# Sliding-window unfold (im2col): nine shifted copies built in SBUF and stored with one transfer per tile, in place of three copies and three strided stores

## Chip, cores and metric

The kernel runs on one core of one Trainium2 chip. The metric is device time in microseconds (us) of one execution, lower is better; the figure for a kernel is the median of its runs. The profile is of one further execution, whose own time is given beside the median.

## The reference

The input `x` is float32 of shape 16 x 64 x 32 x 32 (4.19 MB). For each of the 30 x 30 positions of a 3 x 3 window the nine values under the window are written as a column:

```python
def reference(x, kernel_size):
    batch, c, h, w = x.shape
    h_out = h - kernel_size + 1
    w_out = w - kernel_size + 1
    cols = np.zeros((batch, c * kernel_size * kernel_size, h_out * w_out), dtype=np.float32)
    for b in range(batch):
        col_idx = 0
        for i in range(h_out):
            for j in range(w_out):
                patch = x[b, :, i:i + kernel_size, j:j + kernel_size].copy()
                cols[b, :, col_idx] = patch.ravel()
                col_idx += 1
    return cols
```

So for each of the 16 x 64 = 1024 images the output holds nine rows of 900 numbers, and row (ki, kj) is the 30 x 30 block of the image that begins at row ki and column kj. The output is 1024 x 9 x 900 float32, 33.18 MB. Nothing is calculated; the kernel only moves data.

## The kernel before, in words

An image is one SBUF partition. With 128 partitions there are `n_tiles` = 8 tiles, and the loop at line 47 takes them in turn. For each tile:

- line 51 loads 128 images, 4,096 contiguous bytes each, with one DMA issued from ScalarE's queue (`x_tile`, 512 KB);
- lines 56 to 59 make three copies on VectorE. Copy kj takes all 32 rows of the image and the 30 columns from kj on, and writes them as one contiguous run of 960 numbers, `y_tile[:, kj]`;
- lines 61 to 72 issue three stores from SyncE's queue. Any three rows (0, kj), (1, kj), (2, kj) of the output are the same 960 numbers read from offset 0, 30 and 60, so store kj reads three overlapping runs of 900 numbers per partition out of `y_tile[:, kj]` and writes each to its own place in DRAM:

```python
src = _view(y_tile, kj * (H * WO), [part, [WO, K], [1, HO * WO]])
dst = _view(out, rows0 * out_row + kj * pix, [[out_row, P], [K * pix, K], [1, pix]])
nc.sync.dma_start(out=dst, in_=src)
```

A contiguous run in DRAM is therefore 900 numbers, 3,600 bytes, since the row that follows (ki, kj) in DRAM is (ki, kj+1), which belongs to another store.

Each name in the pool `sbuf` has three buffers (line 45). The framework adds the waits: a copy into `y_tile` of tile t waits until the stores of tile t-3 have landed, a load into `x_tile` of tile t waits until VectorE has copied tile t-3, and store kj waits for copy kj alone. Three queues are at work side by side: ScalarE's with 8 loads and nothing else, VectorE with 24 copies, SyncE's with 24 stores.

Of the kernel before, what the change touches and what calls it, by code (L numbers as in the profile page):

```python
# [2 lines left out]

# [4 lines left out]


def _view(ap: bass.AP, extra_offset: int, dims):
    return dataclasses.replace(
        ap,
        offset=ap.offset + extra_offset,
        ap=[[int(s), int(c)] for s, c in dims],
    )


@with_exitstack
def kernel(  # L20
    ctx: ExitStack,
    tc: tile.TileContext,
    x: bass.AP,
    kernel_size,
    out: bass.AP,
):
    nc = tc.nc
    K = int(kernel_size)
    B, C, H, W = x.shape
    HO = H - K + 1  # L30
    WO = W - K + 1
    assert out.shape == (B, C * K * K, HO * WO)

    P = nc.NUM_PARTITIONS
    dt = x.dtype

    assert P % C == 0
    BPT = P // C
    n_tiles = (B + BPT - 1) // BPT

    x_row = H * W
    out_row = K * K * HO * WO
    pix = HO * WO

    sbuf = ctx.enter_context(tc.tile_pool(name="sbuf", bufs=3))

    for t in range(n_tiles):
        rows0 = t * P
        x_tile = sbuf.tile([P, H * W], dt)
        x_src = _view(x, rows0 * x_row, [[x_row, P], [1, H * W]])  # L50
        nc.scalar.dma_start(out=x_tile, in_=x_src)

        y_tile = sbuf.tile([P, K, H, WO], dt)
        part = y_tile.ap[0]
        xpart = x_tile.ap[0]
        for kj in range(K):
            src = _view(x_tile, kj, [xpart, [W, H], [1, WO]])
            dst = y_tile[:, kj]
            nc.vector.tensor_copy(out=dst, in_=src)  # L59

        for kj in range(K):
            src = _view(
                y_tile,
                kj * (H * WO),
                [part, [WO, K], [1, HO * WO]],
            )
            dst = _view(
                out,
                rows0 * out_row + kj * pix,
                [[out_row, P], [K * pix, K], [1, pix]],  # L70
            )
            nc.sync.dma_start(out=dst, in_=src)  # L72


# [1 line left out]
_INS = ['x', 'kernel_size']  # L76
_OUTS = [((16, 576, 900), 'float32')]
#: Inputs that are plain numbers.
_NUMBERS = {'kernel_size': 3}


# [26 lines left out]
```

## Time and profile before

| | us |
|---|---|
| median of 6 runs | 100.39 |
| lowest and highest of them | 99.64, 100.96 |
| the profiled execution, its own time | 100.73 |
| the span of its trace, from the first to the last instruction | 99.0 |

The page of the profile gives the busy time of each engine, the span in 40 equal slices (a digit is a busy share in tenths, 9 is 90% or more), the DMA queues, the chain of work that ended last, the groups of instructions, and the DMA issues with the time from issue to landing. "q1" is the queue of the stores (SyncE), "q10" that of the loads (ScalarE): their megabytes are those of output and input. A DMA is carried out as packets; their time is given as a share of 16 engines over the stretch. Views asked of the trace for a stretch of time give the same lines for that stretch.

### The profile page before, as it was taken

How to read it: one execution, taken by the hardware profiler on the slowest of the kernel's cores; microseconds unless marked ns; L12 is line 12 of the kernel's file. 1: busy time of each engine (PE TensorE's matmuls, PEld its weight loads, DVE VectorE, ACT ScalarE, POOL GpSimd, SP SyncE). 2: the span in 40 equal slices, each digit the busy share in tenths (PEclk: the TensorE clock that was granted, in tenths of full speed). 3: DMA queues.
4: the chain of work that ended last, by engine and by line, in shares of the span. 5: the costliest groups of instructions: out<-in, count | busy, mean ns of one | idle time of the engine just before them, and what ended most of it. 6: DMA issues, size and time to landing. Idle time of an engine off the chain costs nothing.

```text
span 99.0 us, 138 instructions
## 1 busy us (share of the span) xinstructions
DVE 14.2 (14%) x24; POOL 0.2 (0%) x4
## 2 busy tenths in 40 slices
DVE  0397000006000070001500070007000000000000
POOL 0000000000000000000000000000000000000000
DMA  2999999999999999999999999999999999999981
GB/s 76 369 345 325 340 408 413 419 416 399 399 377 409 412 405 399 385 419 413 405 399 403 403 400 400 399 400 403 400 399 402 402 402 400 400 400 402 399 316 47
DMA packets 10752, 37.37 MB, mean 378 GB/s; under 512 B 512, under 2 KB 512, under 8 KB 10752
## 3 DMA queue, kind: packets, MB, share of 16 engines
q1 hardware_dynamic: 9600, 33.18, 86.2%
q10 hardware_dynamic: 1152, 4.19, 11.3%
HBM read 4.19 MB, written 33.18 MB: 378 GB/s over the span
## 4 chain that ended last, share of the span: by engine, by line
DMA 61%; DVE 7%; DVEq 1%; issue 0%; SPq 0%
DMA out_dram<-y_tile 58%; DVE y_tile L59 7%; DMA x_tile<-in_x_dram 3%; DVEq L103 1%; DVEq L59 0%; SPq L72 0%
## 5 line engine op out<-in xcount | busy, mean ns | idle before, releaser
L59 DVE COPY y_tile<-x_tile 128x960 f32<-128x960 f32 x24 | 14.2, 655 | 54.9 <-DMA out_dram<-y_tile 50.9
L89 POOL MEMSET const-bfloat16-1.0<- 128x1 bf16 x1 | 0.1, 101 | 0.0
L89 POOL MEMSET const-uint8-127<- 128x1 uint8 x1 | 0.1, 101 | 0.0
L89 POOL MEMSET const-float32-0.0<- 128x1 f32 x1 | 0.1, 98 | 0.2 <-issue 0.2
L89 POOL MEMSET const-float32-1.0<- 128x1 f32 x1 | 0.1, 98 | 0.0
## 6 DMA issues: line engine op xcount, KB each, us to landing
out_dram<-y_tile SPq DMA_DIRECT2D x24, 1350.0 KB, 18.8
x_tile<-in_x_dram ACTq DMA_DIRECT2D x8, 512.0 KB, 7.9
```

The costliest lines, as they stand in the source:

```text
L59: nc.vector.tensor_copy(out=dst, in_=src)
L89: nc = _bacc.Bacc("TRN2", target_bir_lowering=False, num_devices=1)
L103: with _tile.TileContext(nc) as tc:
```

## The change

The names `tile_im2col_kernel`, `x_tile` and the loads stay. `y_tile` goes. In its place stands `o_tile`, which holds all nine output rows of an image, 8,100 numbers or 32,400 bytes per partition, in the order of the output. Copy ki writes the three rows (ki, 0), (ki, 1), (ki, 2) in one instruction: its source walks three column offsets, 30 rows and 30 columns, its destination is 2,700 contiguous numbers. Copies ki = 0 and 1 are VectorE's, ki = 2 is ScalarE's. One store per tile then takes the whole of `o_tile`. The old code stays under `PLAN == "A"`, which isn't taken.

```diff
-        y_tile = sbuf.tile([P, K, H, WO], dt)
-        part = y_tile.ap[0]
-        xpart = x_tile.ap[0]
-        for kj in range(K):
-            src = _view(x_tile, kj, [xpart, [W, H], [1, WO]])
-            dst = y_tile[:, kj]
-            nc.vector.tensor_copy(out=dst, in_=src)
-        for kj in range(K):
-            src = _view(
-                y_tile,
-                kj * (H * WO),
-                [part, [WO, K], [1, HO * WO]],
-            )
-            dst = _view(
-                out,
-                rows0 * out_row + kj * pix,
-                [[out_row, P], [K * pix, K], [1, pix]],
-            )
-            nc.sync.dma_start(out=dst, in_=src)
+            o_tile = sbuf.tile([P, K * K, HO * WO], dt)
+            part = o_tile.ap[0]
+            xpart = x_tile.ap[0]
+            for ki in range(K):
+                src = _view(
+                    x_tile,
+                    ki * W,
+                    [xpart, [1, K], [W, HO], [1, WO]],
+                )
+                dst = _view(
+                    o_tile,
+                    ki * K * pix,
+                    [part, [pix, K], [WO, HO], [1, WO]],
+                )
+                if ki < 2:
+                    nc.vector.tensor_copy(out=dst, in_=src)
+                else:
+                    nc.scalar.copy(out=dst, in_=src)
+            dst = _view(
+                out,
+                rows0 * out_row,
+                [[out_row, P], [1, out_row]],
+            )
+            nc.sync.dma_start(out=dst, in_=o_tile)
```

Two queues change their order. The first is ScalarE's. Before, it holds the eight loads alone (`DVE_49` is the count of VectorE's finished instructions, a `DMAHW` name is the count of a landed transfer; the numbers behind `x_tile` tell the tiles apart):

```order
L51 DMA x_tile_58<-in_x_dram 128x1024
L51 DMA x_tile_67<-in_x_dram 128x1024
L51 DMA x_tile_76<-in_x_dram 128x1024
L51 DMA x_tile_85<-in_x_dram 128x1024 [waits DMAHW0_49,DVE_49]
L51 DMA x_tile_94<-in_x_dram 128x1024 [waits DMAHW1_49,DVE_49]
L51 DMA x_tile_103<-in_x_dram 128x1024 [waits DMAHW2_49,DVE_49]
```

After, a table load and eight copies stand among the loads (`Activation_49` is the count of ScalarE's own finished instructions):

```order
L81 DMA x_tile_72<-in_x_dram 128x1024
L100 ACT_TABLE_LOAD
L100 COPY o_tile_60<-x_tile_58 128x2700 [waits DMAHW0_49]
L100 COPY o_tile_67<-x_tile_65 128x2700 [waits DMAHW1_49]
L100 COPY o_tile_74<-x_tile_72 128x2700 [waits DMAHW2_49]
L81 DMA x_tile_79<-in_x_dram 128x1024 [waits DVE_49,Activation_49]
L81 DMA x_tile_86<-in_x_dram 128x1024 [waits DVE_49,Activation_49]
L81 DMA x_tile_93<-in_x_dram 128x1024 [waits DVE_49,Activation_49]
L100 COPY o_tile_81<-x_tile_79 128x2700 [waits DMAHW4_49,DMAHW3_49]
L81 DMA x_tile_100<-in_x_dram 128x1024 [waits DVE_49,Activation_49]
```

The fourth load moved from behind the third load to behind ScalarE's first three copies, and a load waits for two engines in place of one.

The second is SyncE's, the queue of the stores. Before, the first stores read:

```order
L72 DMA out_0_dram<-y_tile_60 384x1x900 [waits DVE_49] x2
L72 DMA out_0_dram<-y_tile_60 384x1x900 [waits DMAHW0_49,DVE_49]
L72 DMA out_0_dram<-y_tile_69 384x1x900 [waits DMAHW1_49,DVE_49]
L72 DMA out_0_dram<-y_tile_69 384x1x900 [waits DMAHW3_49,DVE_49]
L72 DMA out_0_dram<-y_tile_69 384x1x900 [waits DMAHW4_49,DVE_49]
```

After:

```order
L107 DMA out_0_dram<-o_tile_60 128x8100 [waits DVE_49,Activation_49]
L107 DMA out_0_dram<-o_tile_67 128x8100 [waits DVE_49,Activation_49]
L107 DMA out_0_dram<-o_tile_74 128x8100 [waits DMAHW1_49,DVE_49,Activation_49]
L107 DMA out_0_dram<-o_tile_81 128x8100 [waits DMAHW3_49,DVE_49,Activation_49]
L107 DMA out_0_dram<-o_tile_88 128x8100 [waits DMAHW4_49,DVE_49,Activation_49]
```

A tile's three stores of 384 rows of 900 numbers became one of 128 rows of 8,100, and the store that waited for one VectorE copy now waits for all copies of its tile, on two engines.

## Rows read from the trace of the kernel before

**Rows 1.** The page: busy engines, DMA over 40 slices, packets and queues.
```profile
DVE 14.2 (14%) x24; POOL 0.2 (0%) x4
...
DMA  2999999999999999999999999999999999999981
...
DMA packets 10752, 37.37 MB, mean 378 GB/s; under 512 B 512, under 2 KB 512, under 8 KB 10752
...
q1 hardware_dynamic: 9600, 33.18, 86.2%
q10 hardware_dynamic: 1152, 4.19, 11.3%
```

**Rows 2.** The page: chain of work that ended last, shares of the span.
```profile
DMA 61%; DVE 7%; DVEq 1%; issue 0%; SPq 0%
```

**Rows 3.** Waits of the engines: who waited for what, total us, times, longest.
```profile
DVE y_tile L59 <- DMA out_dram<-y_tile: 50.9, 5, 13.9
DVE y_tile L59 <- DMA x_tile<-in_x_dram: 4.0, 1, 4.0
```

**Rows 4.** DMA queues from 50 to 90 us: packets, MB, share of 16 engines.
```profile
DMA packets 4637, 16.02 MB, mean 401 GB/s; under 512 B 186, under 2 KB 186, under 8 KB 4637
...
q1 hardware_dynamic: 4637, 16.02, 102.5%
```

**Rows 5.** DMA queues from 97.55 to 97.65 us, the last small packet.
```profile
DMA packets 1, 0.00 MB, mean 0 GB/s; under 512 B 1, under 2 KB 1, under 8 KB 1
...
q1 hardware_dynamic: 1, 0.00, 0.6%
```

**Rows 6.** DMA queues from 37.5 to 45.5 us, the last load among stores.
```profile
q1 hardware_dynamic: 775, 2.69, 86.1%
q10 hardware_dynamic: 144, 0.52, 16.0%
```

**Rows 7.** Timeline from 0 to 4.7 us: start, us, engine, instructions merged.
```profile
0.33 0.10 POOL L89 MEMSET const-uint8-127<- 128x1 uint8 x1
0.72 1.34 ACTq L51 DMA_DIRECT2D x_tile<-in_x_dram  x3
3.98 1.23 DVE L59 COPY y_tile<-x_tile 128x960 f32<-128x960 f32 x2 [3.98 <-DMA x_tile<-in_x_dram]
4.67 0.60 SPq L72 DMA_DIRECT2D out_dram<-y_tile  x1
```

**Rows 8.** The page: the group of VectorE's copies, busy and mean ns.
```profile
L59 DVE COPY y_tile<-x_tile 128x960 f32<-128x960 f32 x24 | 14.2, 655 | 54.9 <-DMA out_dram<-y_tile 50.9
```

**Rows 9.** DMA queues from 4.6 to 6.03 us, before the first store packet.
```profile
DMA packets 105, 0.39 MB, mean 269 GB/s; under 512 B 11, under 2 KB 11, under 8 KB 105
...
q10 hardware_dynamic: 105, 0.39, 88.9%
```

**Rows 10.** DMA queues from 6.0 to 6.1 us, with the first store packet.
```profile
q10 hardware_dynamic: 13, 0.05, 110.4%
q1 hardware_dynamic: 1, 0.00, 8.8%
```

**Rows 11.** DMA queues from 6.2 to 6.5 us.
```profile
q10 hardware_dynamic: 18, 0.06, 51.3%
q1 hardware_dynamic: 17, 0.06, 51.1%
```

**Rows 12.** The page: DMA issues, KB each, median us from issue to landing.
```profile
out_dram<-y_tile SPq DMA_DIRECT2D x24, 1350.0 KB, 18.8
x_tile<-in_x_dram ACTq DMA_DIRECT2D x8, 512.0 KB, 7.9
```

**Rows 13.** DMA queues from 95.3 us, and from 97.65 us, to the end.
```profile
q1 hardware_dynamic: 121, 0.38, 26.0%
...
DMA packets 0, 0.00 MB, mean 0 GB/s; under 512 B 0, under 2 KB 0, under 8 KB 0
```

More of the change, by code (lines that the diff above doesn't have):

```diff
@@ L8 @@
 from concourse._compat import with_exitstack
+PLAN = "B"
 def _view(ap: bass.AP, extra_offset: int, dims):
@@ L45 @@
     sbuf = ctx.enter_context(tc.tile_pool(name="sbuf", bufs=3))
[L47 to L51, printed above, removed]
-        y_tile = sbuf.tile([P, K, H, WO], dt)
-        part = y_tile.ap[0]
-        xpart = x_tile.ap[0]
-        for kj in range(K):
-            src = _view(x_tile, kj, [xpart, [W, H], [1, WO]])
-            dst = y_tile[:, kj]
-            nc.vector.tensor_copy(out=dst, in_=src)
-        for kj in range(K):
-            src = _view(
-                y_tile,
-                kj * (H * WO),
-                [part, [WO, K], [1, HO * WO]],
-            )
+    if PLAN == "A":
+        for t in range(n_tiles):
+            rows0 = t * P
+            x_tile = sbuf.tile([P, H * W], dt)
+            x_src = _view(x, rows0 * x_row, [[x_row, P], [1, H * W]])
+            nc.scalar.dma_start(out=x_tile, in_=x_src)
+            y_tile = sbuf.tile([P, K, H, WO], dt)
+            part = y_tile.ap[0]
+            xpart = x_tile.ap[0]
+            for kj in range(K):
+                src = _view(x_tile, kj, [xpart, [W, H], [1, WO]])
+                dst = y_tile[:, kj]
+                nc.vector.tensor_copy(out=dst, in_=src)
+            for kj in range(K):
+                src = _view(
+                    y_tile,
+                    kj * (H * WO),
+                    [part, [WO, K], [1, HO * WO]],
+                )
+                dst = _view(
+                    out,
+                    rows0 * out_row + kj * pix,
+                    [[out_row, P], [K * pix, K], [1, pix]],
+                )
+                nc.sync.dma_start(out=dst, in_=src)
+    else:
+        for t in range(n_tiles):
+            rows0 = t * P
+            x_tile = sbuf.tile([P, H * W], dt)
+            x_src = _view(x, rows0 * x_row, [[x_row, P], [1, H * W]])
+            nc.scalar.dma_start(out=x_tile, in_=x_src)
+            o_tile = sbuf.tile([P, K * K, HO * WO], dt)
+            part = o_tile.ap[0]
+            xpart = x_tile.ap[0]
+            for ki in range(K):
+                src = _view(
+                    x_tile,
[6 more added lines that the diff above has]
+                    [part, [pix, K], [WO, HO], [1, WO]],
+                )
+                if ki < 2:
+                    nc.vector.tensor_copy(out=dst, in_=src)
+                else:
+                    nc.scalar.copy(out=dst, in_=src)
```

## Prediction

> **What bounds the kernel now.** I read the page from the top. VectorE, the only engine with real work, is busy for 14.2 us of 99.0, while the slices of the DMA engines stand at 9 from the second to the thirty-eighth [rows 1]. The chain that ended last says the same: 61% of it is DMA [rows 2]. The waits show VectorE standing for 50.9 us behind stores that have to free a buffer [rows 3]; that is an engine kept waiting by the bound, and it costs nothing. From 50 to 90 us the 16 DMA engines carry nothing but stores, at 401 GB/s, and the packets' time adds up to 102.5% of the stretch, so that each packet begins a little before the one ahead of it is over [rows 4]. The kernel is thus a stream of store packets that never runs dry. It can only gain by cheaper packets, and lose by starting the stream later.
>
> **Terms: the packets.** The 9,600 packets of the store queue [rows 1] are 24 stores of 384 runs of 3,600 bytes (9,216) and 16 small ones behind each store (384). Between 50 and 90 us there are 4,637 packets, 186 of them small [rows 4]. One small packet by itself takes 0.6% of 16 x 0.1 us, 9.6 ns [rows 5]. The 4,451 others share 1.025 x 16 x 40 us = 656 us less 186 x 9.6 ns: 147.0 ns each; in wall time 16 x 40 us / 4,451 = 143.8 ns, and 576 per engine make 82.8 us. A load packet carries 4,096 bytes: 16.0% of 16 x 8 us less 16 small ones, over 128, is 158.8 ns [rows 6]. If 9.6 ns is what any packet costs, a load's bytes take (158.8 - 9.6) / 4,096 = 0.0364 ns each. At that rate 3,600 bytes and the 9.6 ns make 140.7 ns, and a store packet has 6.3 ns more.
>
> The changed store has 128 runs of 32,400 bytes, nine times as long, so 64 per engine over eight stores. No row shows such a packet. Its price has these bounds: 9 x 143.8 = 1,294 ns if nothing is saved; 9.6 + 9 x 137.4 = 1,246 ns if only the 9.6 ns are paid once; 9.6 + 32,400 x 0.0364 + 6.3 = 1,196 ns if the 6.3 ns belong to a packet's two ends and are paid once too; 1,190 ns without them. I take 1,197 ns, because the load row, whose packet is the longest shown, is the nearest: 64 x 1,197 ns = 76.6 us, 6.2 us less than now.
>
> By the Trainium skill (DMA: Bandwidth & Descriptors, "Why small descriptors are slow") a packet pays a fixed overhead that fades with its size. It puts it at about three cycles and only worries at 256 bytes and below; the 9.6 ns of the row are more than that, and at 3,600 bytes still 7% of a packet.
>
> **Terms: the start.** Now the first load lands at 3.98 us, the first VectorE copy of 655 ns ends, and the first store is issued at 4.67 us [rows 7, 8]. From then until 6.03 us only loads move, all 105 packets being q10's [rows 9]; a first store packet stands at 6.04 us [rows 10], 1.37 us behind the issue, just as the last packets of the first three loads go (some are still there at 6.2 us [rows 11]). So the load stream covers the wait. After the change the first store waits for two VectorE copies of 2,700 numbers, one behind the other, and a ScalarE copy beside them. The price of such a copy is not in the trace. By numbers alone the row gives 2,700 / 960 x 655 = 1,842 ns; with the 0.10 us of GpSimd's memset of one number per partition as a fixed part [rows 7] it gives 1.66 us. Both hold if the engine goes at the old pace. If it goes at half of it, the same two sums give 3.68 and 3.23 us. The destination is one run as before, but the source is no longer 32 rows of 30; it is three overlapping windows of 30 rows. I take 3.0 us, near the slow end.
>
> That end has a rule behind it. The row's copies take 0.68 ns per number. By the Trainium skill (VectorE: DVE Perf Modes, "What auto-detection actually checks") float32 copies in SBUF move two numbers per cycle only if the outermost counts of source and destination are both even or equal. Before, they are 32 and 960, and 0.68 ns is indeed under one cycle of its 0.96 GHz, so the trace agrees. Now they would be 3 and 2,700 (the destination being one run), neither equal nor both even, so one number per cycle: an estimate of 2,700 x 1.04 ns plus a fixed part of about 0.1 us, 2.9 us.
>
> First store packet: 3.98 + 2 x 3.0 + 0.03 + 1.37 = 11.4 us, that is 5.3 us later than now. With the first three loads gone by about 6.3 us, the DMA engines stand idle for those 5 us; the fourth load can't fill the gap, since ScalarE's queue now has three copies ahead of it.
>
> **Terms that cost nothing.** ScalarE's table load comes behind its third load issue, which ends at 2.06 us [rows 7], and its first copy can't begin before 3.98 us; together with the 6.0 us of VectorE's pair, table load and copy have 7.9 us of cover, and the copy takes 1.7 to 3.7 us by the same bounds. If that cover were gone, each us over it would delay the first store by as much. Loads four to eight sit behind copies: the fourth is issued once ScalarE's third copy is done, at 15 us with 3.7 us each, and lands about 8 us later [rows 12], or some 11 us if it takes turns with packets of 1.2 us, so by 26 us. Its tile is wanted in DRAM only when three stores of 9.6 us are through, after 40 us. Steadily a tile costs VectorE 6 us per 9.6 us of store, and two queued stores cover each refill. SyncE has 8 issues in place of 24.
>
> **The sum.** 11.4 us, plus 76.6 us of stores and 0.1 us of small packets, plus 40 load packets per engine at 158.8 ns, 6.35 us: 94.4 us. The same account of the kernel now, 6.04 + 82.8 + 6.35, gives 95.2 us. The trace has 26.0% of 3.7 us = 0.96 us of packets per engine left at 95.3 us [rows 13], a mean end of 96.3 us; and a last packet at about 97.6 us, since one starts behind 97.55 us and none from 97.65 us on [rows 5, 13]. So 1.1 us are in slower packets and the end of the third load, 1.3 us in engines that end unevenly. I keep 0.9 us of the first and 0.6 us, half a long packet, of the second: 95.9 us. Another 1.4 us pass from the last packet to the end of the span (97.6 to 99.0), giving 97.3 us, and the profiled execution took 1.73 us more than its span: 99.0 us. That is 1.7 us under its 100.73 us; off the median of 100.39 us it makes 98.7 us.
>
> **Rivals.** Each is given against the median.
>
> 1. The copies keep their pace. For: nothing in the instruction but its source pattern differs. Against: that pattern. At 1.84 us the first packet comes at 9.1 us, 2.3 us sooner: 96.4 us.
>
> 2. Slower than before: bytes, not packets, are what DRAM takes, or the long run is cut into short packets again, so that the change doesn't do what it says. Its place is the steady stretch from 12 us on. The late start stays and nothing pays for it. For: 401 GB/s is so steady that it may be DRAM's own rate for writes. Against: load packets, 14% longer, move more bytes per busy ns (25.8 against 24.5). With 1,294 ns per run and 1.3 us of uneven end the time is 98.7 + 6.2 + 0.7 = 105.6 us; with 1,246 ns it is 101.8 us. It decides from where the stores gain under 4.5 us, above 1,224 ns per run.
> A rule of the Trainium skill speaks for this one (DMA: Bandwidth & Descriptors, "Where 436 GB/s comes from"): DRAM gives a core about 358 GB/s, and that binds such transfers. The 401 GB/s are already above it, so here it doesn't hold as a cap; its 435 GB/s for the way into SBUF would, and 16 x 32,400 bytes in 1,197 ns are 433 GB/s.
>
> 3. Refills show: a tile's copies end after the two queued stores, and the DMA slices show gaps of some us per tile. Against: 6 us of work against 19 us of cover. A gap of 1 us in each of five refills gives 103.7 us.
>
> **How the numbers follow.** Forecast 0.60, rival 1 0.15, rival 2 0.22 (a third of it near 1,246 ns), rival 3 0.03. A measurement here tells about 1% from no change, so the borders are 99.4 and 101.4 us. The forecast's own range, with copies of 2.7 to 3.7 us and 1,190 to 1,210 ns per run, is 97.4 to 100.8 us: 0.45 of its 0.60 is faster, 0.13 within 1%, 0.02 slower. Rival 1 is faster. Rival 2 is slower but for 0.01. Rival 3 is split between slower (0.02) and within 1% (0.01). Sums: 0.60, 0.15, 0.25. The range takes in rival 1 and the near end of rival 2 and leaves out its far end: 96.0 to 102.3 us.
>
> **What would show it.** Right: 1,152 store-queue packets (1,024 long, 128 small), a steady rate near 430 GB/s, VectorE copies near 3 us, idle DMA from about 6.3 to 11.4 us, no gap later. Wrong: VectorE copies near 1.8 us (rival 1), a steady 401 GB/s or many more packets (rival 2), low digits between the tiles (rival 3).

## The result and the profile after

The changed kernel takes 97.29 us (median of 10 runs, 97.10 to 97.71); beside it the kernel before takes 100.48 us (20 runs). The ratio is 0.9705, with a 95% interval of 0.9672 to 0.9738: 3.2 us faster, where 1.7 us were forecast. 97.29 us lies in the stated range, and 0.1 us below the forecast's own one of 97.4 to 100.8 us, whose lower end its own terms (2 x 0.3 us and 64 x 7 ns off 98.7 us) put at 97.6 us.

The profiled execution took 97.38 us with a span of 95.6 us. The page of the changed kernel, the lines that answer to [rows 1], the chain for [rows 2], the groups of copies for [rows 8], and the DMA issues for [rows 12]:

```profile
DVE 46.5 (49%) x16; ACT 20.7 (22%) x9; POOL 0.2 (0%) x4
...
DMA  2950788999799988999899989999999999999990
...
DMA packets 2304, 37.37 MB, mean 391 GB/s; under 512 B 256, under 2 KB 256, under 8 KB 1280
...
q1 hardware_dynamic: 1152, 33.18, 80.4%
q10 hardware_dynamic: 1152, 4.19, 11.5%
...
DMA 50%; DVE 21%; DVEq 3%; issue 0%; SPq 0%
...
L98 DVE COPY o_tile<-x_tile 128x2700 f32<-128x2700 f32 x16 | 46.5, 2959 | 25.4 <-DMA out_dram<-o_tile 21.5
L100 ACT COPY o_tile<-x_tile 128x2700 f32<-128x2700 f32 x8 | 19.4, 2445 | 45.7 <-DMA out_dram<-o_tile 45.2
...
out_dram<-o_tile SPq DMA_DIRECT2D x8, 4050.0 KB, 23.5
x_tile<-in_x_dram ACTq DMA_DIRECT2D x8, 512.0 KB, 14.3
```

VectorE works more than three times as long as before, for the same bytes of output, and the kernel is faster: its busy share says nothing here. The store queue has 1,152 packets in place of 9,600, and its packets' time is 80.4% of 95.6 us where it was 86.2% of 99.0 us. Loads land 14.3 us behind their issue in place of 7.9 us, since they take turns with packets of 1.2 us, and past the first load no copy is held up by one. VectorE's part of the chain has grown from 7% to 21%. The new cost stands in the DMA slices: the digits 5 and 0 in the third and fourth slice are the engines waiting for the first tile. The timeline shows that wait, and answers to [rows 7] (start, us, engine, instructions merged):

```profile
2.09 1.28 ACT L100 ACT_TABLE_LOAD   x1 [2.09 <-issue]
3.87 7.14 ACT L100 COPY o_tile<-x_tile 128x2700 f32<-128x2700 f32 x3 [0.49 <-DMA x_tile<-in_x_dram]
3.87 17.33 DVE L98 COPY o_tile<-x_tile 128x2700 f32<-128x2700 f32 x6 [3.87 <-DMA x_tile<-in_x_dram]
9.79 62.50 SPq L107 DMA_DIRECT2D out_dram<-o_tile  x8
9.80 11.84 ACTq L81 DMA_DIRECT2D x_tile<-in_x_dram  x3
```

The first copy begins at 3.87 us, the first store is issued at 9.79 us, two VectorE copies later; ScalarE's copy of that tile is long done. The DMA queues of the same kernel from 6.4 to 9.7 us, from 9.7 to 11.3 us, from 11.3 to 11.5 us, from 68 to 88 us, and the packets that begin from 94.25 us and from 94.35 us on (a view counts a packet, with its whole time, where it begins):

```profile
q10 hardware_dynamic: 16, 0.04, 2.8%
...
q10 hardware_dynamic: 24, 0.10, 32.9%
...
q1 hardware_dynamic: 8, 0.26, 300.0%
...
q1 hardware_dynamic: 293, 8.46, 98.0%
...
DMA packets 5, 0.00 MB, mean 0 GB/s; under 512 B 5, under 2 KB 5, under 8 KB 5
...
DMA packets 0, 0.00 MB, mean 0 GB/s; under 512 B 0, under 2 KB 0, under 8 KB 0
```

The engines are all but idle before the store is issued, then 24 packets of the load issued beside it go first, at 32.9% of 16 x 1.6 us or 351 ns each, the store's first long packets begin behind 11.3 us, and all is over by 94.35 us. The fourth line prices the packet (32 of the 293 are small): 0.98 x 16 x 20 us less 32 x 9.6 ns, over 261, is 1,200 ns for 32,400 bytes.

### The profile page after: what moved, and what is told of

It is laid out like the page before. It is cut to its first block, busy times and chain, and to the rows that moved or that the text cites. A ratio compares the mean times of both kernels' runs of the same rounds, so it can differ in the third digit from the quotient of the medians.

```text
span 95.6 us, 115 instructions
## 1 busy us (share of the span) xinstructions
DVE 46.5 (49%) x16; ACT 20.7 (22%) x9; POOL 0.2 (0%) x4
## 3 DMA queue, kind: packets, MB, share of 16 engines
q1 hardware_dynamic: 1152, 33.18, 80.4%
q10 hardware_dynamic: 1152, 4.19, 11.5%
## 4 chain that ended last, share of the span: by engine, by line
DMA 50%; DVE 21%; DVEq 3%; issue 0%; SPq 0%
DMA out_dram<-o_tile 46%; DVE o_tile L98 21%; DMA x_tile<-in_x_dram 3%; DVEq L138 3%; DVEq L98 0%; SPq L107 0%
## 5 line engine op out<-in xcount | busy, mean ns | idle before, releaser
L98 DVE COPY o_tile<-x_tile 128x2700 f32<-128x2700 f32 x16 | 46.5, 2959 | 25.4 <-DMA out_dram<-o_tile 21.5
L100 ACT COPY o_tile<-x_tile 128x2700 f32<-128x2700 f32 x8 | 19.4, 2445 | 45.7 <-DMA out_dram<-o_tile 45.2
## 6 DMA issues: line engine op xcount, KB each, us to landing
x_tile<-in_x_dram ACTq DMA_DIRECT2D x8, 512.0 KB, 14.3
```

The lines of the kernel that those rows point to most:

```text
L100: nc.scalar.copy(out=dst, in_=src)
```

## The experiments

Seven kernels ran. Each was measured beside the kernel before, which had a median of 100.28 us in the first four and 100.62 us in the last three.

**Short runs again.** The changed copies, and three stores per tile in the old runs of 3,600 bytes:

```diff
-            dst = _view(out, rows0 * out_row, [[out_row, P], [1, out_row]])
-            nc.sync.dma_start(out=dst, in_=o_tile)
+            for kj in range(K):
+                srs = _view(o_tile, kj * pix, [part, [K * pix, K], [1, pix]])
+                dst = _view(out, rows0 * out_row + kj * pix,
+                            [[out_row, P], [K * pix, K], [1, pix]])
+                nc.sync.dma_start(out=dst, in_=srs)
```

Expected:

> The changed kernel with its nine copies, but three stores per tile as before: 384 runs of 3,600 bytes each, all of them waiting for all copies of the tile. Theory (a packet pays a fixed part, and 3,600 bytes are too few to spread it): the first store packet stays at 11.4 us, the steady rate falls back from 434 to 401 GB/s, the stores take 82.8 us in place of 76.8 us, and the time is 97.3 + 6.0 = 103.3 us, or up to 105.7 us if the slower early packets (1.1 us) and the uneven end (1.3 us) of the kernel before come back as well: then those two belong to short runs. Rival (the gain comes from nine rows built side by side in SBUF or from reading them there without overlap, not from the length of a run): the rate stays at 434 GB/s and the time at 97 to 98 us.

Measured: 104.33 us, ratio to before 1.0417 (1.0359 to 1.0476). The timeline of this kernel, with its first store and the load beside it:

```profile
9.91 75.56 SPq L113 DMA_DIRECT2D out_dram<-o_tile  x24
9.91 11.82 ACTq L81 DMA_DIRECT2D x_tile<-in_x_dram  x3
```

And its DMA queues from 10 to 13.1 us, from 12.9 to 13.15 us, from 13.15 to 20 us, from 68 to 88 us, and from 100.4 us to the end:

```profile
q10 hardware_dynamic: 111, 0.45, 65.3%
...
q1 hardware_dynamic: 1, 0.00, 3.5%
...
DMA packets 812, 2.80 MB, mean 409 GB/s; under 512 B 36, under 2 KB 36, under 8 KB 812
...
q1 hardware_dynamic: 2321, 8.01, 102.5%
...
q1 hardware_dynamic: 37, 0.08, 10.0%
```

The share of 102.5% for 2,321 packets gives 147.0 ns per run, to the digit that of [rows 4], and 401 GB/s. So it is the length of a run that made the stores cheap. The rival falls: rows built side by side and read without overlap give nothing by themselves. (That there are 24 stores here in place of 8 is not it either: the next experiment has 24 too. Whether short runs that follow one another in DRAM would cost as much was not tried.) Two things differ from what was expected. The first store packet comes at 13.15 us, 3.2 us behind an issue at 9.91 us; the load issued in the same moment went first, and its packets were slow: 65.3% of 16 x 3.1 us over 111 is 292 ns each, where a load packet of [rows 6] took 158.8 ns. And behind the first store packet the slower packets and most of the uneven end did not come back. 13.15 + 82.8 us and the four loads that were still to come (32 packets per engine, 5.1 us) are 101.0 us; the last row has 0.2 us of packets per engine left at 100.4 us, a mean end of 100.6 us, so the stream has no slower packets left to account for (before: 1.1 us of them and of the third load's end); it runs at 409 GB/s from its first packet on. That matters for the failed step below.

**Three runs of 10,800 bytes.** One store behind each copy:

```diff
-            dst = _view(out, rows0 * out_row, [[out_row, P], [1, out_row]])
-            nc.sync.dma_start(out=dst, in_=o_tile)
+            for ki in (2, 0, 1):
+                dst = _view(out, rows0 * out_row + ki * K * pix,
+                            [[out_row, P], [1, K * pix]])
+                nc.sync.dma_start(out=dst, in_=o_tile[:, ki * K : (ki + 1) * K])
```

Expected:

> The changed kernel with three stores per tile, one for each copy, in runs of 10,800 bytes; each store waits for its own copy alone. Theory (9 ns per packet and 27.2 bytes per ns): a packet takes 406 ns, the stores 78.0 us, 1.2 us more than now; the first store packet comes after one VectorE copy, at 8.2 us in place of 11.4 us; time 97.3 + 1.2 - 3.2 = 95.3 us. Rival (only a whole 32,400-byte row goes at the full rate): 401 GB/s, 82.8 us of stores, 97.3 + 6.0 - 3.2 = 100.1 us.

Measured: 96.75 us, ratio 0.9659 (0.9604 to 0.9714). Its timeline has the first store at

```profile
6.93 63.86 SPq L108 DMA_DIRECT2D out_dram<-o_tile  x24
```

and its DMA queues, from 7.75 to 7.9 us (the first packets), from 12 to 14 us, from 30 to 40 us (loads run among the stores) and from 68 to 88 us, read

```profile
q1 hardware_dynamic: 12, 0.13, 205.0%
...
q1 hardware_dynamic: 69, 0.75, 113.0%
...
q1 hardware_dynamic: 397, 3.77, 88.9%
...
q1 hardware_dynamic: 880, 8.47, 101.1%
```

96 of the 880 packets are small: (1.011 x 16 x 20 us - 0.9 us) / 784 = 411 ns per 10,800 bytes. That is near the 406 ns expected and far from the 431 ns of the rival (three times 143.8), so most of the gain needs no whole row. The 5 ns that they have over 406 ns cost little, for the packets overlap (101.1%): 16 x 20 us less the small ones, over 784, is 407 ns on the clock. Nor do they show where loads run among the stores: 349 of the 397 packets of the third row are long, at 406 ns each. Of the 1.4 us by which the time is above 95.3 us, the second row has 0.5 us: its 69 packets took 524 ns each. Another part is the end, where one engine stops at 93.5 us and the other 15 by 93.2 us.

**Rows outermost.** The same copies with their dimensions in another order:

```diff
-                    [xpart, [1, K], [W, HO], [1, WO]],
+                    [xpart, [W, HO], [1, K], [1, WO]],
...
-                    [part, [pix, K], [WO, HO], [1, WO]],
+                    [part, [WO, HO], [pix, K], [1, WO]],
```

Expected:

> The changed kernel with the dimensions of every copy in another order: 30 rows outermost, then the three column offsets, then 30 columns, on both sides; the same numbers from the same windows. Theory (VectorE goes at half its pace because the outermost counts, 3 and 2,700, are neither equal nor both even; now they are 30 and 30): a VectorE copy takes 1.6 to 1.84 us, the first store packet comes at 8.5 to 9.0 us, time 94.4 to 94.9 us. Rival (the pace is set by the three overlapping windows of the source): 2.96 us per copy and 97.3 us as now.

Measured: 94.62 us, ratio 0.9448 (0.9395 to 0.9501). The copies on its page:

```profile
L98 DVE COPY o_tile<-x_tile 128x2700 f32<-128x2700 f32 x16 | 24.2, 1563 | 43.4 <-DMA x_tile<-in_x_dram 43.4
L100 ACT COPY o_tile<-x_tile 128x2700 f32<-128x2700 f32 x8 | 19.5, 2462 | 43.9 <-DMA x_tile<-in_x_dram 43.9
```

Its first store in the timeline, and its DMA queues from 8 to 10 us:

```profile
7.24 60.72 SPq L107 DMA_DIRECT2D out_dram<-o_tile  x8
...
q1 hardware_dynamic: 32, 1.04, 129.7%
```

The same numbers from the same overlapping windows take 1,563 ns in place of 2,959 ns on VectorE, so the windows are not what slows the copy; the order of its dimensions is. ScalarE's copy stays at 2.46 us. The kernel takes 2.7 us less, where the issue of the first store moved by 2.5 us (9.79 to 7.24 us) and its first packet by 3.2 us (behind 11.3 us to 8.1 us). A part of the missing half us is in the first 32 store packets, at 1,297 ns in place of 1,200 ns each.

**The first tile in pieces.** On top of that order, tile 0 is stored behind each copy, all others whole:

```diff
+            for ki in ((0, 1, 2) if t == 0 else (None,)):
+                lo, n = (0, K * K) if ki is None else (ki * K, K)
+                dst = _view(out, rows0 * out_row + lo * pix,
+                            [[out_row, P], [1, n * pix]])
+                nc.sync.dma_start(out=dst, in_=o_tile[:, lo : lo + n])
```

Expected:

> The kernel with the reordered copies, and for the first tile alone three stores, one behind each copy; all other tiles keep one store. Theory (each us by which the stream of stores starts sooner is a us off the end): first store packet at 6.9 us, time 97.3 - 4.5 = 92.8 us. If the copies keep 2.96 us: first packet at 8.2 us, 94.1 us. Rival (a stream that starts beside the first loads and copies has slower packets, as in the kernel before from 6 to 12 us): about 1 us of this is given back, 93.8 us.

Measured: 93.80 us, ratio 0.9361 (0.9297 to 0.9425). Its first store in the timeline:

```profile
5.71 60.31 SPq L109 DMA_DIRECT2D out_dram<-o_tile  x10
```

Its DMA queues from 9 to 13 us:

```profile
DMA packets 183, 1.53 MB, mean 382 GB/s; under 512 B 16, under 2 KB 16, under 8 KB 57
...
q1 hardware_dynamic: 142, 1.36, 92.2%
q10 hardware_dynamic: 41, 0.17, 10.4%
```

The early start pays, but a us of it is given back, as the rival had it: from 9 to 13 us this kernel moves 382 GB/s although its engines are full (92.2% + 10.4%). The 126 store packets of 10,800 bytes there take 467 ns each in place of 411 ns, which is 0.4 us per engine; the rest of that us is not accounted for.

**All loads first, in the kernel before.** Which of its parts makes that stretch slow?

```diff
-        x_tile = sbuf.tile([P, H * W], dt)
-        x_src = _view(x, rows0 * x_row, [[x_row, P], [1, H * W]])
-        nc.scalar.dma_start(out=x_tile, in_=x_src)
+    xbuf = ctx.enter_context(tc.tile_pool(name="xbuf", bufs=8))
+    x_tiles = []
+    for t in range(n_tiles):
+        x_tile = xbuf.tile([P, H * W], dt)
+        x_src = _view(x, t * P * x_row, [[x_row, P], [1, H * W]])
+        nc.scalar.dma_start(out=x_tile, in_=x_src)
+        x_tiles.append(x_tile)
```

Expected:

> The kernel before with eight buffers for x_tile in a pool of their own and all eight loads issued ahead of everything else; copies and stores as before, in runs of 3,600 bytes. Theory A (the 1.1 us of slower packets and 1.3 us of uneven end that the prediction carried over arise where a new load begins beside the young stream of stores; here no load begins later): the DMA rate from 7 to 12 us rises from 317-346 to about 400 GB/s, the engines end within 1 us of each other, time 100.4 - 1.0 to - 2.0 = 98.4 to 99.4 us. Theory B (mixing loads with stores is the cause, whenever the load was issued): the slow stretch stays and time stays at 100.4 us, or goes up by as much as 1 us, since all loads are now mixed with stores. Theory C (short runs do it by themselves): time stays at 100.4 us and the slow stretch stays.

Measured: 100.05 us, ratio 0.9947 (0.9918 to 0.9977): half a us less, a small change that is none of the three answers. Its first store in the timeline:

```profile
4.76 4.37 SPq L78 DMA_DIRECT2D out_dram<-y_tile  x3
```

Its DMA queues from 4.8 to 9.35 us (no packet of q1) and from 6 to 10 us:

```profile
q10 hardware_dynamic: 371, 1.38, 92.6%
...
DMA packets 347, 1.26 MB, mean 314 GB/s; under 512 B 38, under 2 KB 38, under 8 KB 347
...
q10 hardware_dynamic: 331, 1.20, 94.6%
q1 hardware_dynamic: 16, 0.06, 3.6%
```

For comparison, the DMA queues of the kernel before from 7 to 12 us:

```profile
DMA packets 469, 1.68 MB, mean 336 GB/s; under 512 B 16, under 2 KB 16, under 8 KB 469
```

No store packet begins before 9.35 us, 4.6 us behind its issue: the backlog of loads goes first. And the loads, alone on the engines, are slow too: 314 GB/s from 6 to 10 us. So mixing loads with stores (theory B) is not needed for the slow stretch, nor are short runs (theory C; the second experiment's packets of 10,800 bytes were slow from 12 to 14 us), nor a load that begins later (theory A, whose price of 1 to 2 us isn't there). What makes packets slow in the first 14 us stays open.

**Two pieces, and two pieces with all loads first.** The first tile as 10,800 and 21,600 bytes; then the same with the loads ahead, by the edit above:

```diff
-            for ki in ((0, 1, 2) if t == 0 else (None,)):
-                lo, n = (0, K * K) if ki is None else (ki * K, K)
+            for lo, n in ((0, K), (K, 2 * K)) if t == 0 else ((0, K * K),):
```

Expected of two pieces:

> As the kernel with the reordered copies and the first tile's store split, but in two pieces, 10,800 bytes behind the first VectorE copy and 21,600 bytes behind the other two copies. Theory (a packet pays 9 ns, and each of the 10,800-byte ones of the first tile had 28 ns more): eight packets per engine fewer and eight of the slower kind fewer, first packet still at 6.6 us, time 93.8 - 0.1 to - 0.4 = 93.4 to 93.7 us. Rival (the slow stretch belongs to the moment, not to the packets): 93.8 us as before.

Expected with all loads first:

> The two-piece kernel with all eight loads issued ahead of everything else, from eight buffers. Theory A (a load that begins beside the young store stream costs it time): the 0.4 to 0.7 us of slow packets go, time 93.0 to 93.3 us. Theory B (mixing is the cause): time as the two-piece kernel's or up to 1 us more, since the store of the first tile now shares the engines with five loads in place of one or two; ScalarE's first copy also comes 1.5 us later behind five more load issues, which the first piece of the store should cover.

Measured: 93.36 us (93.21 to 94.42), ratio 0.9307 (0.9267 to 0.9347), and 94.54 us, ratio 0.9400 (0.9376 to 0.9425). The two pieces have the best median of all, but their interval overlaps that of the three; the two can't be told apart, and so neither can theory and rival. Loads first lose 1.2 us, which theory A excludes and theory B puts at 1 us at most. The two-piece kernel's first stores in the timeline:

```profile
5.60 7.74 SPq L108 DMA_DIRECT2D out_dram<-o_tile  x4
```

Its DMA queues from 5.6 to 6.45 us (no store packet yet), from 6.45 to 6.6 us, from 10 to 12 us and from 12 to 14 us (packets of 21,600 bytes in the last two):

```profile
q10 hardware_dynamic: 66, 0.23, 65.2%
...
q1 hardware_dynamic: 11, 0.12, 187.4%
...
q1 hardware_dynamic: 33, 0.69, 92.2%
...
q1 hardware_dynamic: 32, 0.69, 80.4%
```

The stream of stores begins 4.8 us sooner than the changed kernel's, and its time is 3.9 us less (3.4 us between the two profiled executions, 93.98 against 97.38 us). Here too packets are slow for a while: 32 of 21,600 bytes take 922 ns each from 10 to 12 us, and 804 ns from 12 to 14 us.

With all loads first the store is issued at 5.54 us, but its DMA queues from 5.6 to 9.6 us hold loads alone:

```profile
DMA packets 319, 1.18 MB, mean 294 GB/s; under 512 B 32, under 2 KB 32, under 8 KB 319
...
q10 hardware_dynamic: 319, 1.18, 98.8%
```

These are slow again, at 294 GB/s, as in the kernel before with its loads first.

## Why the prediction was right, and where its size came from

*The bound* was read rightly: a stream of store packets that only cheaper packets or a later start could move. VectorE's work grew from 14.2 to 46.5 us, and nothing of it shows in the time but the first 6 us.

*The packets.* Taken 1,197 ns, measured 1,200 ns, so 76.8 us for the stores. Of the four bounds the third was right in size, though not in its parts: the 6.3 ns that a 3,600-byte packet has over the load row's price come in a stretch of stores alone, where packets overlap to 102.5%. With loads among them the same packets took 141 ns, as the kernel before shows from 16 to 18 us (10 of the 134 are small):

```profile
q1 hardware_dynamic: 134, 0.45, 54.9%
```

That is the load row's price without the 6.3 ns.

The first experiment puts the whole term on the run's length, which rival 2 denied: 401 GB/s was not DRAM's rate for writes. The 358 GB/s of the Trainium skill (DMA: Bandwidth & Descriptors, "Where 436 GB/s comes from") fall further behind, and 16 x 32,400 bytes in 1,200 ns, 432 GB/s, are just under its 435 GB/s.

*The start.* Taken 3.0 us per copy and 11.4 us for the first long packet; measured 2,959 ns and a packet behind 11.3 us. That VectorE would go at half its pace was chosen as the slow end of the rows. The third experiment shows that the order of the dimensions decides: with 30 and 30 outermost the same copy takes 1,563 ns. By the rule of the Trainium skill cited ahead (VectorE: DVE Perf Modes, "What auto-detection actually checks") 3 and 2,700 forbid two numbers per cycle and 30 and 30 allow it; both measurements agree. That these counts and nothing else in the order decide was not tried by itself; the pace is in any case a matter of writing and not of the work. Rival 1 fell for the kernel as it was changed, and its first half, a faster copy, holds for the reordered one.

*What cost nothing.* The table load (1.28 us, over at 3.4 us) and ScalarE's copy of 2,445 ns were covered, as said. No gap stands between tiles (rival 3): from the fifth slice to the last but one no digit of the DMA engines is under 7.

*The step that failed* is the last of the sum: "I keep 0.9 us of the first and 0.6 us, half a long packet, of the second". The account up to 94.4 us came out, in part by luck: the stores took 0.2 us more than was taken, and 24 load packets, 0.2 us per engine, had moved before the first store packet. The last packet ended not at 95.9 us but by 94.35 us, so neither the slower packets nor the uneven end carried over.

For keeping 0.9 of the 1.1 us the prediction gives no reason. About 0.36 us of them were the end of the third load, which by its own account is over before the new stream starts. Another 0.2 us arose at 28 to 30 us. The kernel before shows both, the packets of q10 from 6.04 us on and those of q1 from 28 to 30 us:

```profile
q10 hardware_dynamic: 771, 2.77, 7.5%
...
q1 hardware_dynamic: 172, 0.59, 85.6%
```

The 2.77 MB are 676 load packets, 36 more than the account's 640, and 165 of the 172 store packets are long, at 166 ns each. The rest is, on balance, slow packets in the first 13 us. Every trace here has such a stretch between 4 and 14 us, on whatever moves then: stores beside loads (the kernel before, 336 GB/s from 7 to 12 us; the three pieces, 467 ns in place of 411 ns), stores alone or nearly so (three runs, 524 ns in place of 411 ns; rows outermost, 1,297 ns in place of 1,200 ns; the two pieces, 922 ns and then 804 ns), and loads alone (the two kernels with all loads first, 314 and 294 GB/s). The changed kernel and the first experiment have it as well, at 351 and 292 ns per load packet in place of 158.8 ns, but ahead of their first store packet, where the sum begins. So the changed kernel paid 5.3 us for the late start, as forecast, and its stream escaped the slow stretch, which the sum had charged to it. What makes those packets slow is open.

The uneven end is open too. It was 1.3 us from the mean to the last packet before and 0.6 us in the first experiment (100.6 to 101.2 us); in the changed kernel all engines end between 93.9 and 94.35 us. But in the trace of the two pieces, whose packets are as long but for the first tile's, one engine ends at 90.9 us and the other 15 by 90.2 us. So long packets do not ensure an even end.

The two ends of the run, 1.3 us from the last packet to the end of the span and 1.78 us outside it, came as forecast (1.4 and 1.73 us).

## What to carry to other kernels

When a stream of transfers never runs dry, price its packets one by one: a small packet of the trace gives the fixed part, the longest one the part per byte, and a longer contiguous run is worth the fixed part that it saves. Building a whole tile for that run delays the first store; split the first tile alone, and write the copies so that both sides have equal or even outermost counts (here together 3.9 us more). Before adding a remainder of the old trace to the new sum, ask when it arose and on which packets: what is slow at one moment of the execution costs only the stream that runs then.

## What the runs showed of the hardware that was not expected

- A transfer's first packet depends on what was issued on the other queue. With no load under way, or the end of one, it comes 0.9 us after its issue (6.93 to about 7.8 us, three runs; 5.60 to about 6.5 us, two pieces); with a load issued in the same moment 1.5 to 3.2 us after it, behind slow load packets (9.79 to 11.3 us, changed kernel; 9.91 to 13.15 us, short runs); behind a backlog of loads at least 4.6 us after it (4.76 to 9.35 us).
- With loads among the stores, packets of 3,600, 10,800 and 32,400 bytes take 141, 406 and 1,200 ns, and a fixed part of about 9 ns with 36.8 ns per 1,000 bytes fits all three. In a stream of stores alone the two shorter ones take 147 and 411 ns but overlap, so that they come to 143.8 and about 407 ns on the clock. What those few ns are is open.
